# A hybrid SSD and attention layer on one core: silu moved to the projections and built from tanh, z loaded apart, group statistics taken a span later, a third product bank in the scan

## The chip, the core and the metric

The kernel runs on one core of a Trainium2 chip. The metric is the device time of one execution in microseconds; lower is better. The core's engines run side by side and meet through semaphores: TensorE (PE) multiplies matrices into the PSUM memory (8 banks of 512 float32 columns by 128 partitions), VectorE (DVE), ScalarE (ACT) and GpSimd (POOL) work elementwise, and SyncE (SP) issues the DMAs. Each engine takes its instructions in the order in which the built program has them.

## What is computed

One step of a layer for a 1024-frame prompt and a 64-frame continuation, laid side by side as T = 1088 columns. The parts that matter here:

```python
xn = _rmsnorm(x, p['norm_mix_w'])
proj = xn @ p['w_in']
z, xbc, dt_raw, q, k, v, gate_ssm, gate_att = jnp.split(proj, ...)
xbc_c, conv_new = _causal_dwconv(conv_past, xbc, p['ssm_conv_w'], p['ssm_conv_b'])
xbc_c = jax.nn.silu(xbc_c)
xs, bm, cm = jnp.split(xbc_c, ...)
y_ssm, ssm_new = _ssd_scan(xs, dt, a_neg, bm, cm, ...)      # chunk by chunk, 32 heads in 4 groups
y_ssm = y_ssm + p['ssm_d'] * xs
y_ssm = y_ssm * jax.nn.silu(z)
y_ssm = _rmsnorm(y_ssm by group, p['ssm_norm_w'])
o = differential attention over q, k, v (chunk-causal; the continuation sees 512 cached keys)
mix = sigmoid(gate_ssm) * (y_ssm @ w_branch_ssm) + sigmoid(gate_att) * (o @ w_branch_attn)
x = x + mix @ w_out
x = x + (silu(conv(h_a)) * h_b) @ w_down                     # h = RMSNorm(x) @ w_up
```

`silu(a)` is `a * sigmoid(a)`, which equals `(a/2) * (tanh(a/2) + 1)`.

## The kernel before, in words

**Products.** Every weight product is made from float32 numbers split into a high and a low part, as three matmuls per 128-row block (L148 to L150). One product of 128 output rows by 384 or 320 columns (the three parts of T in `WIDE`) is 24 matmuls and fills one PSUM bank. `acc` (L112) hands out the banks: two banks `mm` of the pool `pm`, and, while `more` is a pool, three further banks `mx`. `more` is set from L225 to L410, that is for the norm and for the projections of V, Q and K; after that there are two banks only. The piece that evacuates a bank must have read it to the end before the second-next product may begin in it.

**Stages.** First the norm of x and the projections of V and dt, then Q and K (`heads`, L312). When the 8 tiles of K are projected, `heads` scales all eight rows on DVE (L343 and L346), turns two of them by the rotary tables (L352 to L357), splits each into high and low (L307 and L308) and stores them. Beside this PE already works on the *stream* (`stream`, L465): the projections of z (`z_tiles`), of the convolution inputs x, B, C (`conv_tiles`) and of the gates (`gate_tiles`), in the order of `ORDER` (L67): four tiles of z, six of the convolution, sixteen of the gates, and so on. A z piece is copied from its bank by ACT (L429) and stored to `z_sc`. A convolution piece is copied by ACT into `pre` (L447), multiplied by the first tap (L456), three more taps follow on DVE (L458), and `cc` is stored to `x_sc`.

**Attention** (L483 to L642) goes head by head; each of its 72 units is followed by 1.9 pieces of the stream (`fill`). **The scan** (L645 to L774) runs over 12 spans: 4 groups by the 3 parts of T. `fetch` (L646) loads one span's B, C, four tiles of x and four of z into one tile `in`; `gate` (L655) applies silu to all ten, five at a time, on ACT (L658) and then loads the table set `natural_log_exp_and_others` (L660), which has Ln and Exp. `step` (L663) is one chunk of 128: the decays `bc` (a DMA that spreads 8 rows to all partitions, L668), transposes `tr` and `cb` on PE, Exp on ACT (L672, L687), the products `yi`, `ye` and the state update `stp`. `gated` (L717), at each span's end, adds the skip term, multiplies by the gated z on POOL, squares on ACT, sums on POOL, and then at once takes the group statistics with the ones matrix into a bank of its own, `gst` (L727), with Ln, Exp and Square on ACT (`rstd_of`, L206), the scaling on DVE (L731) and the store to `y_sc` (L732). The scan has six banks (`tr`, `cb`, `yi`, `ye`, `stp`, `gst`), each with one buffer. After every step and after `gated` 1.65 pieces are filled in: what is left of the stream, then, from the fifth span on, the attention branch product (`branch`, L161) and the first half of the SSM branch product. For the last chunk of each group the initial state is loaded at the place where it is needed (L695).

After the scan come the second half of the SSM branch (from groups 2 and 3 of `y_sc`), the output product with the second norm (L794 to L822, `rstd_of` again), and the feed-forward part, which is the rest of the time.

**Order.** The program is written with tiles in pools; a scheduler places the instructions of all engines. It takes the instructions roughly as written, evacuations and weight loads ahead of others (`tc.high_priority`), and moves an instruction up where its inputs come early. SP issues all DMAs in one queue.

## Time and profile before

| | us |
|---|---|
| median of 3 runs | 2575.67 |
| lowest, highest run | 2572.8, 2580.09 |
| the profiled execution, its own time | 2576.31 |
| span of the profiled execution (first to last instruction) | 2574.2 |
| PE busy in that span | 2525.0 |
| DVE, ACT, POOL busy | 1321.2, 1074.9, 288.3 |

"Busy" of PE is the union of its matmuls, which overlap; 15924 of them were recorded. The stages in the trace, by the time from the span's start: norm and V to about 100, Q and K to about 335, z and convolution alone to about 408, attention to about 1110, the scan to about 1600, the rest of the branches to about 1700, the output product to about 1790, the feed-forward part to the end. A row of the table of groups has the line, engine, operation, out<-in, partitions x elements and count, then busy microseconds and the mean nanoseconds of one, then the idle time of the engine just before.

### The profile page before, as it was taken

The page shows a single profiled execution, that of the slowest core. Times are in us where ns is not written, and L with a number is a line of the kernel's source. Part 1 is how long each engine was busy: PE and PEld are TensorE (multiplying, and loading weights), DVE is VectorE, ACT ScalarE, POOL GpSimd, SP SyncE. Part 2 cuts the span into 40 slices and gives each one's busy share as a digit, 9 for nine tenths or more (in the row PEclk, how much of TensorE's full clock was granted, in tenths as well). Part 3 has the DMA queues.
Part 4 walks back from the last instruction along what each step waited for, and adds up shares of the span by engine and source line. Part 5 has one row for each costly group of instructions (what it writes and reads, how often), then busy time and mean ns, then how long its engine had stood idle before and what let it go on. Part 6 is the DMA issues. An engine that isn't in the chain of part 4 may idle for free.

```text
span 2574.2 us, 40564 instructions
## 1 busy us (share of the span) xinstructions
PE 2525.0 (98%) x15924; PEld 2440.6 (95%) x15924; DVE 1321.2 (51%) x2238; ACT 1074.9 (42%) x2219; POOL 288.3 (11%) x393
## 2 busy tenths in 40 slices
PE   8999999999999999999989999999999999999999
PEld 8999998999999999988889889999999999999999
DVE  6326256655447674567556656657333333333333
ACT  6234344544445454478655664235313122221221
POOL 3000001000000110025233222022000000000000
PEclk9999999999999999999999999999999999999999
DMA  5217167545345434265795746666311111111111
GB/s 161 79 58 283 52 253 212 155 136 155 113 134 167 118 121 128 65 197 191 224 307 184 232 149 194 196 192 195 119 42 50 42 48 44 42 50 39 44 44 77
DMA packets 216352, 340.40 MB, mean 132 GB/s; under 512 B 28225, under 2 KB 164673, under 8 KB 216033
## 3 DMA queue, kind: packets, MB, share of 16 engines
q1 hardware_dynamic: 216160, 337.81, 41.7%
q8 instruction: 125, 2.05, 0.3%
q14 instruction: 67, 0.54, 0.1%
HBM read 237.60 MB, written 100.13 MB: 131 GB/s over the span
## 4 chain that ended last, share of the span: by engine, by line
PE 47%; DMA 5%; ACT 2%; DVE 1%; issue 1%; SPq 0%; POOL 0%; DVEq 0%; ACTq 0%; POOLq 0%
PE mm L148 8%; PE mm L150 8%; PE mm L149 8%; PE up L148 7%; PE up L149 7%; PE up L150 7%; DMA bc<-a_sc 1%; PE yi L692 1%; DMA b_f<-y_sc 1%; PE stp L705 1%; PE ye L699 1%; DMA in<-x_sc 1%; ACT bc L687 0%; DVE w_lo L142 0%; DVE b_lo L173 0%
## 5 line engine op out<-in xcount | busy, mean ns | idle before, releaser
L148 PE MATMUL mm<-xn_hi,w_hi 128*128 128x320 f32 (+1 forms) x1496 | 499.5, 334 | 5.1 <-ACT zr L429 4.1
L150 PE MATMUL mm<-xn_hi,w_lo 128*128 128x320 f32 (+1 forms) x1496 | 498.4, 333 | 0.0
L149 PE MATMUL mm<-xn_lo,w_hi 128*128 128x320 f32 (+1 forms) x1496 | 494.4, 331 | 0.0
L142 DVE TENSOR_TENSOR w_lo<-w_f,w_hi 128x1024 fp32r<-128x1024 f32 (+2 forms) x196 | 247.9, 1265 | 301.4 <-ACT w_hi L141 298.7
L141 ACT CAST w_hi<-w_f 128x1024 fp32r<-128x1024 f32 (+2 forms) x196 | 203.9, 1041 | 458.9 <-PE mm L149 297.5
L148 PE MATMUL up<-x_hi,w_hi 128*128 128x384 f32 (+1 forms) x1056 | 344.3, 327 | 1.3 <-ACT x_hi L821 1.3
L149 PE MATMUL up<-x_lo,w_hi 128*128 128x384 f32 (+1 forms) x1056 | 344.1, 326 | 0.0
L150 PE MATMUL up<-x_hi,w_lo 128*128 128x384 f32 (+1 forms) x1056 | 342.4, 326 | 0.0
L148 PEld LDWEIGHTS mm<-xn_hi,w_hi 128*128 128x128 f32 x1496 | 282.2, 189 | 11.7 <-ACT zr L429 5.0
L150 PEld LDWEIGHTS mm<-xn_hi,w_lo 128*128 128x128 f32 x1496 | 282.0, 188 | 3.8 <-issue 2.6
L149 PEld LDWEIGHTS mm<-xn_lo,w_hi 128*128 128x128 f32 x1496 | 282.2, 189 | 2.5 <-issue 1.2
L148 PE MATMUL mm<-b_hi,w_hi 128*128 128x384 f32 (+1 forms) x576 | 196.4, 341 | 9.1 <-ACT b_g L188 4.5
L148 PEld LDWEIGHTS up<-x_hi,w_hi 128*128 128x128 f32 x1056 | 198.1, 188 | 1.7 <-ACT x_hi L821 1.6
L149 PEld LDWEIGHTS up<-x_lo,w_hi 128*128 128x128 f32 x1056 | 198.2, 188 | 0.1
L150 PEld LDWEIGHTS up<-x_hi,w_lo 128*128 128x128 f32 x1056 | 198.0, 188 | 0.0
L150 PE MATMUL mm<-b_hi,w_lo 128*128 128x384 f32 (+1 forms) x576 | 193.2, 336 | 2.2 <-DVE w_lo L142 2.2
L149 PE MATMUL mm<-b_lo,w_hi 128*128 128x384 f32 (+1 forms) x576 | 192.7, 335 | 0.0
L881 DVE TENSOR_TENSOR xa<-xa,mm 128x384 f32<-128x384 f32 x144 | 76.5, 531 | 197.3 <-PE mm L150 197.3
L149 PE MATMUL mm<-f_lo,w_hi 128*128 128x384 f32 (+1 forms) x528 | 173.1, 328 | 0.0
L148 PE MATMUL mm<-f_hi,w_hi 128*128 128x384 f32 (+1 forms) x528 | 173.0, 328 | 0.0
L150 PE MATMUL mm<-f_hi,w_lo 128*128 128x384 f32 (+1 forms) x528 | 172.9, 328 | 0.0
L458 DVE SCALAR_TENSOR_TENSOR cc<-pre,par,cc 128x384 f32<-128x384 f32 (+1 forms) x216 | 128.4, 595 | 45.3 <-ACT cc L456 42.2
(253 smaller groups left out, 4741.0 us busy)
## 6 DMA issues: line engine op xcount, KB each, us to landing
w_f<-in_win_dram SPq DMA_DIRECT2D x76, 512.0 KB, 3.8
w_f<-in_wup_dram SPq DMA_DIRECT2D x44, 512.0 KB, 3.6
bc<-a_sc SPq DMA_DIRECT2D x32, 512.0 KB, 5.0
w_f<-in_wout_dram SPq DMA_DIRECT2D x24, 512.0 KB, 3.6
x_sc<-cc SPq DMA_DIRECT2D x48, 192.0 KB, 1.9
kh_t<-k_st SPq DMA_DIRECT2D x32, 272.0 KB, 7.9
kl_t<-k_st SPq DMA_DIRECT2D x32, 272.0 KB, 7.5
w_f<-in_wbs_dram SPq DMA_DIRECT2D x16, 512.0 KB, 4.5
```

What stands on the lines that cost most here:

```text
L141: S.copy(hi, w)
L142: V.tensor_tensor(out=lo, in0=w, in1=hi, op=ALU.subtract)
L148: PE.matmul(ps, a_hi, b_hi, start=i == 0, stop=False)
L149: PE.matmul(ps, a_hi, b_lo, start=False, stop=False)
L150: PE.matmul(ps, a_lo, b_hi, start=False, stop=i == n - 1)
L458: V.scalar_tensor_tensor(cc[:, :m], pre[:, i : i + m], cw(i), cc[:, :m], ALU.mult, ALU.add)
L692: PE.matmul(yi[u : u + 64, e // 2, :L], xdt[:L, e], bc[:L, e, :L], start=True, stop=True)
L699: PE.matmul(ye[:, j, :L], state[:, P * j : P * (j + 1)], bx[:, 1, cs], start=True, stop=True)
L705: PE.matmul(up, b_cb[:L, :P], xw[:L].rearrange("p e q -> p (e q)"), start=True, stop=True)
L881: V.tensor_tensor(out=xa[:, m, c : c + w], in0=xa[:, m, c : c + w], in1=ps, op=ALU.add)
```

## The change

1. **silu at the projections.** A z piece is no longer copied: ACT writes `tanh(z/2)` from the bank into `zr`, and a new DVE instruction makes `(zr + 1) * ps`, which reads the bank a second time. A convolution piece gets, after its taps, a Tanh on ACT (written into `pre`) and a DVE instruction `(pre + 1) * cc`. The convolution's taps and biases are halved beforehand and the norm weights of the SSM group norm are scaled to make up for z's factor 2 (`rstd_of` gets 0.25/512).
2. **No gate in the scan.** `gate`, with its Silu and its two table loads, is gone. z has a tile of its own, `zin`.
3. **Statistics a span later.** `gated` stops after the sums; the rest, `normed`, runs after the third step of the next span, and for the last span after the scan's last piece. Its bank is no longer `gst` but `cb`, which the steps use.
4. **A third product bank.** The bank that this frees becomes `mx`, a third bank of `acc` for the length of the scan.
5. `bc` has four buffers for three; the initial state is loaded once per group, when the group starts, into a tile `start`.

In the built program of after the table loads stand so: one before the first Tanh, Ln and Exp at the end of K's projection, then a pair (one for Ln, one for the Exp or Tanh behind it) at each of the 12 statistics of the scan, and a pair at each of the three statistics of the output product. The convolution and z pieces of the attention stage run Tanh beside Exp without a load.

```diff
@@ -45,7 +45,6 @@
 QR = 10
 QSQ = 1
 BF = 3
-GATE_AT = 2
 UPB = 5
 NXR = 4
 NSQ = 3
@@ -56,7 +55,6 @@
 ZR = 3
 ATT_STEPS = 1.9
 SCAN_STEPS = 1.65
-SPLIT = 5
 BRANCH_AT = 4
 
 
@@ -107,12 +105,13 @@
 
     pm = ctx.enter_context(tc.tile_pool(name="pm", bufs=2, space=PSUM))
 
-    more, at_bank = None, 0
+    more, at_bank = (None, 0), 0
 
     def acc(w):
         nonlocal at_bank
-        at_bank = (at_bank + 1) % 5
-        pool, tag = (more, "mx") if more is not None and at_bank < 3 else (pm, "mm")
+        pool, n = more
+        at_bank = (at_bank + 1) % (n + 2)
+        pool, tag = (pool, "mx") if at_bank < n else (pm, "mm")
         t = pool.tile([P, 512], F32, name=tag, tag=tag)
         return t[:, :w]
 
@@ -222,7 +221,7 @@
 
     s1 = ExitStack()
     ps1 = s1.enter_context(tc.tile_pool(name="ps1", bufs=1, space=PSUM))
-    more = s1.enter_context(tc.tile_pool(name="psx", bufs=3, space=PSUM))
+    more = s1.enter_context(tc.tile_pool(name="psx", bufs=3, space=PSUM)), 3
 
     def stat(w):
         t = ps1.tile([P, 512], F32, name="st", tag="st", bufs=3)
@@ -243,8 +242,8 @@
                     load(out=con, in_=cst)
             if x == 0:
                 load(out=par, in_=prm)
-                for a, b in ((O_MIX, O_CW), (O_SN, O_D), (O_QN, O_FW)):
-                    V.tensor_scalar_mul(par[:, a:b], par[:, a:b], -1.0)
+                for a, b, by in ((O_MIX, O_CW, -1.0), (O_CW, O_SN, 0.5), (O_SN, O_D, -0.5), (O_QN, O_FW, -1.0)):
+                    V.tensor_scalar_mul(par[:, a:b], par[:, a:b], by)
             for k in range(KT):
                 sq = nx.tile([P, max(NORM)], F32, name="nsq", tag="nsq", bufs=NSQ)
                 if k % 2:
@@ -407,7 +406,7 @@
             split_out(ck, j, PAST, c_st)
         heads(B_K, lambda j: col(O_KN + j), k_st, kT)
     s1.close()
-    more = None
+    more = None, 0
     ahead = AHEAD
     extra.release()
     extra = None
@@ -426,7 +425,8 @@
         for j in tiles:
             def evac(ps, c, w):
                 zr = staged("zr")[:, :w]
-                S.copy(zr, ps)
+                act(zr, ps, AF.Tanh, scale=0.5)
+                V.scalar_tensor_tensor(zr, zr, 1.0, ps, ALU.add, ALU.mult)
                 load(out=z_sc[P * j : P * (j + 1), c : c + w], in_=zr)
 
             yield from project(win[B_Z + j], evac)
@@ -456,6 +456,8 @@
                 act(cc[:, :m], pre[:, :m], AF.Identity, bias=col(O_CB + f), scale=cw(0))
                 for i in range(1, 4):
                     V.scalar_tensor_tensor(cc[:, :m], pre[:, i : i + m], cw(i), cc[:, :m], ALU.mult, ALU.add)
+                act(pre[:, :m], cc[:, :m], AF.Tanh)
+                V.scalar_tensor_tensor(cc[:, :m], pre[:, :m], 1.0, cc[:, :m], ALU.add, ALU.mult)
                 load(out=x_sc[P * f : P * (f + 1), c : c + n], in_=cc[:, :n])
                 if n < w:
                     load(out=x_sc[P * f : P * (f + 1), c + n : c + w], in_=cc[:, n + 3 : m])
@@ -643,28 +645,22 @@
 
 
     with tc.tile_pool(name="sp", bufs=1) as sp, tc.tile_pool(name="pss", bufs=1, space=PSUM) as pss:
+        more = pss, 1
         def fetch(g, c, w):
-            t = sp.tile([P, 10, 384], F32, name="in", tag="in", bufs=2)
+            t = sp.tile([P, 6, 384], F32, name="in", tag="in", bufs=2)
+            z = sp.tile([P, 4, 384], F32, name="zin", tag="zin", bufs=2)[:, :, :w]
             four = slice(4 * P * g, 4 * P * (g + 1))
             for u in range(2):
                 load(out=t[:, u, :w], in_=x_sc[P * (16 + 4 * u + g) : P * (17 + 4 * u + g), c : c + w])
-            for u, d in ((2, x_sc), (6, z_sc)):
-                load(out=t[:, u : u + 4, :w], in_=d[four, c : c + w].rearrange("(j p) t -> p j t", p=P))
-            return t
-
-        def gate(t, w, after=None):
-            with tc.issue_after(after.ins) if after is not None else ExitStack():
-                for u in range(0, 10, SPLIT):
-                    last = act(t[:, u : u + SPLIT, :w], t[:, u : u + SPLIT, :w], AF.Silu)
-            with tc.issue_after(last.ins):
-                S.preload_act_table_set(LN_EXP)
-            return t[:, 0:2], t[:, 2:6], t[:, 6:10, :w]
-
-        def step(g, ch, o, bx, xs, y, state):
+            for d, src in ((t[:, 2:, :w], x_sc), (z, z_sc)):
+                load(out=d, in_=src[four, c : c + w].rearrange("(j p) t -> p j t", p=P))
+            return t[:, 0:2], t[:, 2:6], z
+
+        def step(g, ch, o, bx, xs, y, state, start):
             L = P if ch < 8 else TS
             c0, cs = P * ch, slice(o, o + L)
             h8 = slice(8 * g, 8 * g + 8)
-            bc = sp.tile([P, 8, P], F32, name="bc", tag="bc", bufs=3)
+            bc = sp.tile([P, 8, P], F32, name="bc", tag="bc", bufs=4)
             load(out=bc[:, :, :L], in_=a_sc[h8, c0 : c0 + L].unsqueeze(0).to_broadcast([P, 8, L]))
             e2 = sp.tile([P, 4, P], F32, name="e2", tag="e2", bufs=2)
             for u in range(2):
@@ -684,15 +680,14 @@
             V.tensor_tensor(out=xx[:L], in0=tr3, in1=dtt[:L, :, ch, h8].unsqueeze(3).to_broadcast([L, 2, 8, 64]), op=ALU.mult)
             G.affine_select(bc[:L, :, :L], bc[:L, :, :L], [[0, 8], [1, L]], ALU.is_ge, -1e30, base=0, channel_multiplier=-1)
             for e in range(8):
-                last = act(bc[:L, e, :L], bc[:L, e, :L], AF.Exp, bias=nacum[:L, ch, 8 * g + e : 8 * g + e + 1])
+                act(bc[:L, e, :L], bc[:L, e, :L], AF.Exp, bias=nacum[:L, ch, 8 * g + e : 8 * g + e + 1])
             V.tensor_tensor(out=bc[:L, :, :L], in0=bc[:L, :, :L], in1=b_cb[:L, P : P + L].unsqueeze(1).to_broadcast([L, 8, L]), op=ALU.mult)
             yi = pss.tile([P, 4, P], F32, name="yi", tag="yi")
             for e in range(8):
                 u = 64 * (e % 2)
                 PE.matmul(yi[u : u + 64, e // 2, :L], xdt[:L, e], bc[:L, e, :L], start=True, stop=True)
             if ch == 8:
-                state = sp.tile([P, 512], F32, name="state", tag="state", bufs=2)
-                load(out=state, in_=st0[:, 512 * g : 512 * (g + 1)])
+                state = start
             if state is not None:
                 ye = pss.tile([P, 4, P], F32, name="ye", tag="ye")
                 for j in range(4):
@@ -712,43 +707,48 @@
                 V.tensor_tensor(out=new, in0=new, in1=up, op=ALU.add)
             if ch >= 7:
                 load(out=ssm[ch - 7, :, 512 * g : 512 * (g + 1)], in_=new)
-            return new, last
+            return new
 
         def gated(g, c, w, xs, zt, y):
-            rows = slice(4 * P * g, 4 * P * (g + 1))
-            part = lambda d: d[rows, c : c + w].rearrange("(j p) t -> p j t", p=P)
             for j in range(4):
                 V.scalar_tensor_tensor(y[:, j], xs[:, j, :w], col(O_D + 4 * g + j), y[:, j], ALU.mult, ALU.add)
             G.tensor_tensor(out=y, in0=y, in1=zt, op=ALU.mult)
             act(zt, y, AF.Square)
             G.tensor_tensor(out=zt[:, 0:2], in0=zt[:, 0:2], in1=zt[:, 2:4], op=ALU.add)
             G.tensor_tensor(out=zt[:, 0], in0=zt[:, 0], in1=zt[:, 1], op=ALU.add)
-            ps = pss.tile([P, 512], F32, name="gst", tag="gst")[:, :w]
+
+        def normed(g, c, w, xs, zt, y):
+            rows = slice(4 * P * g, 4 * P * (g + 1))
+            part = lambda d: d[rows, c : c + w].rearrange("(j p) t -> p j t", p=P)
+            ps = pss.tile([P, 512], F32, name="gst", tag="cb")[:, :w]
             PE.matmul(ps, ones, zt[:, 0], start=True, stop=True)
             rs = sp.tile([P, 384], F32, name="grs", tag="grs", bufs=2)[:, :w]
-            rstd_of(sp, rs, ps, w, "gn", 1.0 / 512)
+            rstd_of(sp, rs, ps, w, "gn", 0.25 / 512)
             for j in range(4):
                 V.scalar_tensor_tensor(y[:, j], y[:, j], col(O_SN + 4 * g + j), rs, ALU.mult, ALU.mult)
             load(out=part(y_sc), in_=y)
 
         def scan():
             spans = [(g, c, w) for g in range(4) for c, w in WIDE]
-            raw = fetch(*spans[0])
-            ready = [gate(raw, spans[0][2])]
+            got, due = [fetch(*spans[0])], None
             for i, (g, c, w) in enumerate(spans):
                 if c == 0:
                     state = None
+                    start = sp.tile([P, 512], F32, name="start", tag="start")
+                    load(out=start, in_=st0[:, 512 * g : 512 * (g + 1)])
                 if i + 1 < len(spans):
-                    raw = fetch(*spans[i + 1])
-                bx, xs, zt = ready[i]
+                    got.append(fetch(*spans[i + 1]))
+                bx, xs, zt = got[i]
                 y = sp.tile([P, 4, 384], F32, name="y", tag="y", bufs=2)
                 for o in range(0, w, P):
-                    state, last = step(g, (c + o) // P, o, bx, xs, y, state)
-                    if o == P * GATE_AT and i + 1 < len(spans):
-                        ready.append(gate(raw, spans[i + 1][2], last))
+                    state = step(g, (c + o) // P, o, bx, xs, y, state, start)
+                    if o == 2 * P and due is not None:
+                        normed(*due)
                     yield i
-                gated(g, c, w, xs, zt, y[:, :, :w])
+                due = g, c, w, xs, zt, y[:, :, :w]
+                gated(*due)
                 yield i
+            normed(*due)
 
         def stage():
             return bs.tile([P, 384], F32, name="b_f", tag="b_f", bufs=BF)
@@ -771,6 +771,7 @@
             fill(SCAN_STEPS)
         load(out=conv, in_=conv_o)
         run(filler)
+    more = None, 0
     dq.release()
```

## The prediction

> **What bounds the kernel now.** I read the page's head first, then the busy times by stretches of 100 us, then what PE waits for in the scan, then the clock in shorter stretches. The page:
>
> ```profile
> span 2574.2 us, 40564 instructions
> PE 2525.0 (98%) x15924; PEld 2440.6 (95%) x15924; DVE 1321.2 (51%) x2238; ACT 1074.9 (42%) x2219; POOL 288.3 (11%) x393
> ```
>
> PE is busy in all but 49.2 us. The profiled execution took 2576.31 us, 2.1 more than its span, and stands 0.6 above the median of 2575.67; the sum below is made against it. So an edit that takes time off ACT or DVE is worth only the PE idle time that it ends, and the PE clock that this idle time costs. Where that is, the stretches show (length, then busy us and instructions of PE, PEld, DVE, ACT, POOL, then the granted clock, DMA share and GB/s):
>
> ```profile
> 800.00:900.00 100.00, 100.00 (x646) 97.17 (x645) 71.47 (x152) 53.70 (x131) 11.08 (x37) 1.00 0.51 144
> 1100.00:1200.00 100.00, 96.81 (x655) 86.57 (x654) 70.66 (x88) 75.17 (x153) 39.14 (x33) 1.00 0.61 196
> 1200.00:1300.00 100.00, 94.25 (x622) 83.83 (x622) 58.96 (x68) 70.35 (x133) 36.73 (x25) 0.98 0.75 238
> 1300.00:1400.00 100.00, 93.19 (x619) 84.52 (x618) 58.84 (x82) 60.06 (x113) 30.20 (x21) 0.97 0.78 257
> 1400.00:1500.00 100.00, 90.72 (x559) 80.44 (x559) 62.55 (x86) 67.23 (x137) 27.21 (x19) 0.91 0.60 192
> 1500.00:1600.00 100.00, 99.90 (x660) 91.55 (x657) 66.16 (x90) 51.36 (x104) 30.36 (x19) 1.00 0.53 168
> 2000.00:2100.00 100.00, 100.00 (x606) 100.00 (x605) 36.30 (x57) 20.75 (x32) 2.65 (x8) 1.00 0.15 47
> ```
>
> In the feed-forward part PE is never idle: 606 matmuls in 100 us, so 165 ns from one to the next and 4.0 us for a product of 24. In attention it is nearly so, even where DVE is 71% busy. The scan, 1100 to 1600, holds 25.1 us of PE idle time, half of all there is. Who ended it (waits of PE from 1105 to 1615: us in total, times, longest):
>
> ```profile
> PE mm L148 <- ACT b_g L188: 4.5, 1, 4.5
> PE mm L148 <- ACT zr L429: 4.1, 4, 2.1
> PE ye L699 <- DMA state<-in_st_dram: 3.2, 2, 2.6
> PE mm L148 <- DVE b_g L190: 2.8, 1, 2.8
> PE tr L675 <- ACT in L658: 2.3, 3, 1.5
> PE stp L705 <- ACT b_cb L680: 1.9, 3, 0.9
> ```
>
> These are 18.8 us; eight smaller ones of that answer add 7.9, together 26.7. And the clock (stretches of 25 us, same columns; the ones with a clock under 1):
>
> ```profile
> 1225.00:1250.00 25.00, 21.13 (x135) 18.34 (x134) 15.08 (x21) 18.95 (x33) 7.05 (x5) 0.95 0.60 185
> 1250.00:1275.00 25.00, 25.00 (x163) 22.90 (x162) 13.55 (x16) 16.39 (x28) 8.12 (x7) 0.99 0.72 227
> 1300.00:1325.00 25.00, 19.81 (x130) 17.40 (x129) 11.48 (x18) 13.17 (x23) 3.25 (x5) 0.86 0.99 326
> 1425.00:1450.00 25.00, 20.86 (x131) 17.36 (x131) 20.00 (x32) 17.13 (x30) 2.65 (x2) 0.91 0.87 284
> 1450.00:1475.00 25.00, 25.00 (x155) 22.09 (x154) 11.97 (x21) 18.99 (x47) 11.41 (x7) 0.89 0.61 194
> 1475.00:1500.00 25.00, 20.47 (x125) 18.59 (x125) 11.32 (x16) 18.44 (x31) 3.80 (x4) 0.86 0.51 168
> ```
>
> The clock falls where PE stood idle for 4 us or more, and what it takes is 25 us times 0.05, 0.01, 0.14, 0.09, 0.11 and 0.14: 13.5 us. So at most 40 us can be won in the scan.
>
> **The change part by part.**
>
> *The gate goes (ACT in the scan).* The rows of ACT from 1105 to 1615, costliest first:
>
> ```profile
> L687 ACT ACTIVATE bc<-bc,nacum 128x128 f32<-128x128 f32 (+1 forms) x288 | 86.7, 384 | 19.2 <-POOL bc L685 18.7
> ...
> L658 ACT ACTIVATE in<-in 128x1920 f32<-128x1920 f32 (+1 forms) x24 | 40.6, 1714 | 1.5 <-DMA in<-x_sc 1.2 <-DMA in<-z_sc 0.2
> L658 ACT ACT_TABLE_LOAD x14 | 18.0, 1283 | 35.9 <-DMA in<-x_sc 35.9
> L660 ACT ACT_TABLE_LOAD x12 | 15.4, 1283 | 0.2
> ...
> L210 ACT ACTIVATE gn<-gst,eps_t 128x384 f32<-128x384 f32 (+1 forms) x12 | 6.7, 558 | 7.8 <-PE gst L727 7.7
> ```
>
> 40.6 us of silu leave ACT, and 26 table loads of 1.283 us. The 12 pairs of loads that the built program now has at the statistics put 24 back, so the loads cancel. But the lump goes: two silus and their two loads held ACT about 6.0 us at a time (2 x 1.714 + 2 x 1.283), and the copies that free the product banks, `zr` and `b_g`, and the copy `b_cb` queued behind it. I count the waits for b_g L188, zr, `in` and b_cb as ended by this: 4.5 + 4.1 + 2.3 + 1.9 = 12.8 us. What is late next in these places is the chain through `bc`, which the freer ACT shortens and the fourth buffer of `bc` starts earlier.
>
> *Early state:* the two waits for `state<-in_st_dram`, 3.2 us. Its DMA now stands on SP at the group's start and waits there for the previous group's last chunk to have read `start`; behind it wait that group's loads of `in` and `bc` and a weight block, all of which are wanted later. The load of `zin` likewise waits for the statistics of two spans before, with the same behind it. I cost both at nothing, as two loads of `bc` are ahead by then; if that lead is gone, it is the last rival's price. *Third bank:* an evacuation may be 4.0 us later than before; the one wait for b_g L190, 2.8 us, is shorter than that and goes. Ended in all: 18.8 of 26.7 us. The eight smaller ones (the state, weights, `bc`) I let stay. Of the clock I keep the loss at 1300 to 1325, 3.5 us, where the DMA share is 0.99, and take off the other 10.0. **Scan: -28.8 us.** Bounds: only the 4.5 and 2.3 that name silu's lump at first hand with half of the clock, about -10; all 40 us.
>
> *z's second pass at the end of K's projection.* This is the part that costs. The nearest rows for the new instructions: Tanh from a bank, the old copy, and the same DVE form from a bank:
>
> ```profile
> L420 ACT ACTIVATE gt<-mm 128x384 f32<-128x384 f32 x32 | 15.8, 493 | 31.7 <-PE mm L150 31.6
> L429 ACT COPY zr<-mm 128x384 f32<-128x384 f32 x32 | 15.1, 474 | 27.5 <-PE mm L150 17.6 <-issue 9.0 <-ACT p_t L557 0.8
> L190 DVE SCALAR_TENSOR_TENSOR b_g<-b_g,mm 128x384 f32<-128x384 f32 x16 | 8.8, 551 | 15.0 <-PE mm L150 10.8 <-DMA b_g<-g_sc 4.1
> ```
>
> The duration is nothing: 0.49 for 0.47 us on ACT and 0.55 on DVE. But the bank is now freed by DVE, and for z's first four tiles there are two banks and DVE is the engine that finishes K (time order, DVE):
>
> ```profile
> 342.26 7.67 DVE L343 SCALAR_TENSOR_TENSOR qr<-qr,par,qrs 128x1088 f32<-128x1088 f32 x6
> 349.85 2.61 DVE L346 SCALAR_TENSOR_TENSOR qr<-qr,par,qrs 128x1088 f32<-128x1088 f32 x2
> 352.37 1.28 DVE L308 TENSOR_TENSOR ql<-qr,qh 128x1088 fp32r<-128x1088 f32 x1
> 353.57 1.22 DVE L142 TENSOR_TENSOR w_lo<-w_f,w_hi 128x1024 fp32r<-128x1024 f32 x1
> ```
>
> In the built order of the changed program the DVE instruction of z's second piece stands ahead of these ten, that of the third behind them: 342.26 to 354.79 is 12.5 us in which no bank comes free. PE can spend 4.0 us of it on the fourth piece, in the bank that the second left; the fifth needs the third's bank and waits 12.5 + 0.5 - 4.0 = 9.0 us. Two later evacuations stand behind the rotary products and further splits, for which I add 1 us each. Such an idle stretch also drops the clock, as at 1475 to 1500, where 4.5 idle us go with 3.5 us of lost clock; part of that falls into the wait itself, and I take 2. **+13 us.** The order says the same: between the last statistics of K and the first score product it had 426 stream matmuls and has 344; 82 times 165 ns are 13.5 us. Below: 0 if the start of attention, which waits for K's stores, has as much slack; above: 18.
>
> *The rest of the pieces.* 72 convolution pieces get about 0.5 us of ACT and 0.55 of DVE, 48 z pieces 0.55 of DVE: some 65 us of DVE, most of it in attention, where 800 to 900 shows PE full at DVE 71%. The cover is the filler in PE's queue; bank holding doesn't change for the convolution. I take +2. If nothing covered it, each of some 80 pieces would cost its 0.55: +44; since PE idles not at all in 800 to 900, with DVE as full as it will be elsewhere, I keep 0 to 15. The one more scaling of parameters at the start, 120 columns once, I take at nothing.
>
> *Statistics later, and without the preloaded set.* Between spans nothing waits. Two places have nothing behind them: the last statistics of the scan, and the last of the output product, where PE waits already (waits of PE over the whole span, the first one for the rival below, then the chain of waits by time):
>
> ```profile
> PE sc L543 <- ACT p_t L557: 3.8, 1, 3.8
> ...
> PE up L148 <- ACT x_hi L821: 1.3, 1, 1.3
> ```
>
> ```profile
> 1598.95 5.79 DMA y_sc<-y
> 1604.81 3.19 DMA b_f<-y_sc
> ```
>
> Both chains get two table loads, 2.57 us, of which the first may fall in a gap of ACT: +2 at the output product, +3 at the scan's end, where the built order also has 8 matmuls fewer behind the statistics. Bounds 1 to 7 together. Here the Trainium skill speaks against the change. ScalarE: Activation LUTs, section "Table sets: the hidden batching unit", says that Ln and Exp share the set natural_log_exp_and_others, one load for both, and that calls are to be batched by set; the change gives up just that. Its section "What ACT_TABLE_LOAD costs" has 2.66 us for a switch with the drain, by which these two places would cost 5.3 us each and the forecast be some 5 us higher; the rows above have 1.283 and next to no idle time around it, and I go by them.
>
> **Sum:** -28.8 + 13 + 2 + 5 = -9 us: 2576.3 - 9 = **2567 us**, own range 2558 to 2575. (About 0.3%, 7.7 us, is what a measurement of this kernel can tell from no change.)
>
> **The rivals.**
>
> *The wait at K's end is hidden.* Attention's first scores wait for K's stores anyway, and among the waits is one of 3.8 us on `p_t`, at attention's start. If the idle time only takes their place, or all scan waits go, 9 to 20 us more are won: **2553**. Against it: the 82 matmuls that leave this stretch.
>
> *New waits in the scan.* The waits named were each ended by one engine, but the four-bank chain of transposes, decays and states is in one queue on PE, and the order is new. With half of the gain lost (14 us), the sum is +5: **2579**, no change.
>
> *The shared bank `cb` is held too long, and the kernel gets slower.* From the end of `gst` to the DVE instruction that reads the mean last the bank is taken: two loads 2.57, Ln, Exp and Square at 0.56 each, DVE 0.55, 4.8 us, and in the built order up to five Exps of 0.384 stand between: 6.7. The next `cb` transpose stands 32 to 79 stream matmuls later, which at 165 ns is 5.3 to 13 us, with two or three of the scan's own products beside. So it decides from a hold of some 7 us on: if ACT is kept by Exps whose `bc` lands late, PE stops in order, with all products behind it. 2.5 us at each of 11 spans are 27 us, which with the -9 gives +18: **2594**. For it: those Exps wait 18.7 us for `bc` by the row above; against it: most spans have 40 matmuls and more between, and ACT has 40 us less to do.
>
> **Chances.** Forecast 0.42, more won 0.15, no change by new waits 0.22, slower by the bank 0.21. The forecast's own range is on both sides of -0.3% (2568.6 from the profiled time): 0.27 of it below. Faster 0.45 with a little of the others, same 0.32, slower 0.23. The range leaves out the outer parts of the first and last rival: 2546 to 2590.
>
> **What would show it.** After should have: no wait for L658 or `state<-in_st_dram`; PE idle in the scan under 12 us; a wait of `mm` on DVE `zr` of some 9 us about 350 us after the start, with the clock under 1 behind it; `up <- x_hi` at 3 to 4 us. Waits of PE's `cb` on ACT or DVE `gn` would speak for the bank, waits of `po` or `sc` on DVE `cc` for a dearer attention; no PE idle time at 350 would fell the largest cost of the sum.

## The result, and the profile after

The changed kernel takes **2584.71 us** (median of 11 runs, 2580.46 to 2587.9), the kernel before 2575.67 (now 11 runs, of which the table above has the first three): the ratio is **1.0033, interval 1.0024 to 1.0042**. It is some 9 us slower, where 9 us faster was forecast. The page's head, to set beside that of before:

```profile
span 2581.3 us, 40809 instructions
...
PE 2520.2 (98%) x15924; PEld 2437.3 (94%) x15924; DVE 1381.9 (54%) x2359; ACT 1072.2 (42%) x2271; POOL 287.6 (11%) x393
```

PE now stands idle for 61.1 us instead of 49.2. Where, outside the scan, the changed kernel's stretches of 100 us show, with the same columns as before:

```profile
300.00:400.00 100.00, 90.35 (x532) 88.76 (x531) 51.32 (x76) 37.13 (x60) 0.29 (x2) 0.97 0.54 197
400.00:500.00 100.00, 97.08 (x611) 92.01 (x610) 79.30 (x171) 59.81 (x150) 10.47 (x34) 1.00 0.65 175
...
1700.00:1800.00 100.00, 93.88 (x558) 91.36 (x557) 64.56 (x86) 54.23 (x80) 31.14 (x22) 0.99 0.64 203
```

Of the kernel before, the stretch from 400 and the one from 1700, not shown yet:

```profile
400.00:500.00 100.00, 94.08 (x583) 89.33 (x582) 64.93 (x136) 48.77 (x125) 9.92 (x29) 0.98 0.68 178
...
1700.00:1800.00 100.00, 98.07 (x590) 96.61 (x589) 69.73 (x97) 48.46 (x79) 30.81 (x22) 1.00 0.64 202
```

The reader should compare the counts of matmuls, for a stretch with more of them has done more of the program. Where K ends, 300 to 400, 71 fewer; at attention's start, 400 to 500, 28 more; at the output product, 1700 to 1800, 32 fewer. In the scan, one stretch from 1105 to 1630 gives before and then after:

```profile
1105.00:1630.00 525.00, 497.54 (x3236) 448.31 (x3235) 333.00 (x443) 330.69 (x650) 163.22 (x114) 0.97 0.66 213
```

```profile
1105.00:1630.00 525.00, 496.49 (x3272) 450.73 (x3271) 358.37 (x487) 292.50 (x633) 161.50 (x116) 0.98 0.68 214
```

ACT has lost 38 us of work, but PE's idle time is 28.5 us where it was 27.5. The scan, where 29 us were to be won, does 36 matmuls more, which at 525/3236 = 162 ns each is some 6 us. What PE waits for in the changed kernel, over the whole span (us, times, longest), and then in the scan's stretch:

```profile
PE mm L147 <- DVE zr L429: 10.3, 3, 8.4
...
PE up L147 <- ACT x_hi L822: 3.9, 1, 3.9
```

```profile
PE stp L700 <- ACT b_cb L676: 4.6, 2, 2.7
PE mm L149 <- DVE w_lo L141: 4.1, 4, 1.9
PE mm L147 <- ACT b_hi L171: 2.9, 2, 2.0
PE mm L147 <- DVE b_g L189: 2.5, 1, 2.5
PE mm L148 <- DVE b_lo L172: 2.0, 1, 2.0
```

The waits for silu's `in` and for the state's DMA are gone as forecast; others of the same size stand in their place. Two that were counted as ended are still there: the one for ACT's `b_cb`, 4.6 us where it was 1.9, and the one for DVE's `b_g`, which the third product bank was to end, 2.5 us where it was 2.8 (L189 is L190 of before).

### The profile page after: what moved, and what is told of

Its sections match the earlier page's. It is cut to its first block, busy times and chain, and to the rows that moved or that the text cites. A ratio compares the mean times of both kernels' runs of the same rounds, so it can differ in the third digit from the quotient of the medians.

```text
span 2581.3 us, 40809 instructions
## 1 busy us (share of the span) xinstructions
PE 2520.2 (98%) x15924; PEld 2437.3 (94%) x15924; DVE 1381.9 (54%) x2359; ACT 1072.2 (42%) x2271; POOL 287.6 (11%) x393
## 4 chain that ended last, share of the span: by engine, by line
PE 68%; DVE 5%; DMA 5%; ACT 3%; issue 2%; SPq 1%; POOL 0%; DVEq 0%; ACTq 0%; POOLq 0%
PE mm L149 12%; PE mm L147 12%; PE mm L148 12%; PE up L147 7%; PE up L148 7%; PE up L149 7%; PE po L593 3%; PE sc L546 2%; PE sc L545 1%; PE pt L574 1%; DVE w_lo L141 1%; DMA b_f<-y_sc 1%; PE yi L688 1%; DVE y L728 1%; PE stp L700 1%
## 5 line engine op out<-in xcount | busy, mean ns | idle before, releaser
L147 PE MATMUL mm<-xn_hi,w_hi 128*128 128x384 f32 (+1 forms) x1416 | 472.7, 334 | 13.4 <-DVE zr L429 10.3
L149 PE MATMUL mm<-xn_hi,w_lo 128*128 128x384 f32 (+1 forms) x1416 | 470.8, 333 | 0.6 <-DVE w_lo L141 0.6
L148 PE MATMUL mm<-xn_lo,w_hi 128*128 128x384 f32 (+1 forms) x1416 | 468.7, 331 | 0.0
L147 PEld LDWEIGHTS mm<-xn_hi,w_hi 128*128 128x128 f32 x1416 | 267.5, 189 | 18.3 <-DVE zr L429 11.6
L149 PEld LDWEIGHTS mm<-xn_hi,w_lo 128*128 128x128 f32 x1416 | 267.3, 189 | 3.8 <-issue 1.9
L148 PEld LDWEIGHTS mm<-xn_lo,w_hi 128*128 128x128 f32 x1416 | 267.4, 189 | 2.8 <-issue 1.4
L147 PE MATMUL mm<-b_hi,w_hi 128*128 128x384 f32 (+1 forms) x448 | 149.6, 335 | 7.9 <-ACT b_hi L171 2.9
L149 PE MATMUL mm<-b_hi,w_lo 128*128 128x384 f32 (+1 forms) x448 | 148.1, 331 | 3.5 <-DVE w_lo L141 3.5
L148 PE MATMUL mm<-b_lo,w_hi 128*128 128x384 f32 (+1 forms) x448 | 148.1, 331 | 2.0 <-DVE b_lo L172 2.0
L559 ACT ACTIVATE p_t<-sc,mx 128x1024 f32<-128x1024 f32 (+5 forms) x144 | 106.2, 740 | 87.9 <-DVE mx L550 39.7
```

The source lines that it names most:

```text
L147: PE.matmul(ps, a_hi, b_hi, start=i == 0, stop=False)
L148: PE.matmul(ps, a_hi, b_lo, start=False, stop=False)
L149: PE.matmul(ps, a_lo, b_hi, start=False, stop=i == n - 1)
L559: act(p_t[:n, :nk], sc[c][:n, :nk], AF.Exp, bias=mx[:n, c : c + 1], accum_out=dst)
```

## The experiments

**Theory**: taking silu out of the scan wins there what was forecast or most of it, the ends of K's projection and of the output product cost what was forecast or more, and the statistics' new place (late, in the C.B bank, with the third product bank) takes the scan's gain back. **Rival**: the scan's waits are merely replaced, so that silu's removal wins nothing, whatever the statistics do. Times of different groups of runs are compared by their ratio to the kernel before, 0.1% being 2.6 us.

### The statistics' place, taken apart

*Silu alone* has parts 1, 2 and 5 of the change, with the statistics as before. Its edit, as all that follow, is against the changed kernel (`...` stands for lines left out):

```diff
-        more = pss, 1
...
-            ps = pss.tile([P, 512], F32, name="gst", tag="cb")[:, :w]
+            ps = pss.tile([P, 512], F32, name="gst", tag="gst")[:, :w]
...
-                    if o == 2 * P and due is not None:
-                        normed(*due)
...
                 gated(*due)
+                normed(*due)
                 yield i
-            normed(*due)
```

> The changed kernel with the group statistics taken at once again, in a bank gst of their own, and no third product bank in the scan; silu stays at the projections, z stays apart. Theory A (the scan's waits moved to DVE and DMA, whatever the banks): the scan is as long as in both others and the time within 4 us of 2584.7. Theory B (the new order with the shared bank took back what the missing silu gave): the scan loses 10 us or more of waits and the time is 2570 to 2576. Theory C (the third bank did help): it is slower, 2588 or more.

Measured: 2570.11 us, ratio 0.9976 [0.9967, 0.9985]. In the scan's stretch:

```profile
1105.00:1630.00 525.00, 507.33 (x3349) 460.35 (x3348) 351.89 (x501) 295.91 (x639) 160.41 (x116) 0.99 0.69 218
```

That is 113 matmuls more than before, 18 us. So the rival falls: silu's removal, together with part 5, from which no run parts it, wins in the scan, though 18 and not 29 us, for PE still idles 17.7 us there. The rest of the change loses it again. Four kernels part this rest.

*Late statistics alone* (a span later, bank of their own, no third bank): the changed kernel with

```diff
-        more = pss, 1
...
-            ps = pss.tile([P, 512], F32, name="gst", tag="cb")[:, :w]
+            ps = pss.tile([P, 512], F32, name="gst", tag="gst")[:, :w]
```

> silu_alone (2570.1) with the group statistics a span later, in a bank gst of their own, and no third product bank: the lateness alone. Theory L (the lateness holds z's tile and bunches the work of two spans, so that it costs what silu_alone won over the full change): 2580 to 2585. Theory B (the third bank or the shared bank cost it): 2568 to 2573.

*Shared bank alone*: silu alone with `tag="cb"`. *Third bank at once*: that with `more = pss, 1` too.

> silu_alone with the statistics at once, as there, but in the bank cb that the steps use, and no third product bank (one bank stays empty): the sharing alone. Theory C (PE waits for the mean to be read before the next transposes, the rival on the shared bank): 2578 or more, with waits of cb on DVE gn of some us. Theory B (the third bank): 2568 to 2573. Theory L: as theory B here.

> The changed kernel with the statistics at once: bank cb shared and the third product bank there, only the lateness taken away. Theory B (the third bank lets products run ahead of the scan's chain and of the weights): 2580 to 2585, with waits of products on w_lo, b_lo and b_hi as in the changed kernel. Theory L: 2568 to 2573. Theory C: 2578 or more and equal to shared_bank_only.

Measured: late statistics alone 2574.96 us, 0.9994 [0.9983, 1.0005]; shared bank alone 2593.27, 1.0072 [1.0055, 1.0089]; with the third bank 2600.64, 1.0099 [1.0082, 1.0116]. So lateness costs some 5 us (its interval just meets that of silu alone), which is between its two theories. The shared bank, with statistics at once, costs 25 us by the ratios, as theory C of its run had it. How, its waits in the scan's stretch and its stretch itself show:

```profile
PE mm L147 <- ACT b_hi L171: 13.1, 2, 11.9
PE gst L723 <- POOL zin L717: 8.0, 2, 5.9
PE cb L672 <- DVE gn L212: 5.2, 2, 3.7
```

```profile
1105.00:1630.00 525.00, 485.31 (x3198) 438.53 (x3196) 335.51 (x473) 292.46 (x632) 169.45 (x118) 0.96 0.66 208
```

PE stops in order at `gst`, whose sums POOL has not finished, and at the next `cb`, whose bank DVE has not read out; in silu alone, with a bank of its own, neither stands in that list. The largest wait, 13.1 us for `b_hi`, is taken up below. The view of the tile `cb` says who waited for it (us, times): silu alone first, then the shared bank.

```profile
who waited for it (us, times):
  ACT b_cb L675: 7.4, 7
```

```profile
who waited for it (us, times):
  ACT b_cb L675: 39.4, 18
```

ACT waits 39.4 us for the C.B products instead of 7.4. This is ACT's idle time and not yet time of the kernel: late statistics in the bank of `ye`, below, have 15.7 us of it and cost no more than late statistics in their own bank, which have 5.3. What it leads to is seen in PE's order. In silu alone the C.B products of 1 to 4 chunks of later spans stand ahead of the statistics of each span but the last. In shared bank alone none does, at any of the 12 spans: the next span can't start before the statistics of this one are out of the bank. The scan gets longer, its last statistics run at 1611.8 us instead of 1576.8, and by then PE has no other product ahead of those that need their result. The stretch behind, silu alone first, then the shared bank, and PE's longest wait in it:

```profile
1580.00:1655.00 75.00, 70.72 (x422) 69.07 (x421) 49.98 (x92) 20.80 (x36) 0.00 (x0) 1.00 0.68 209
```

```profile
1580.00:1655.00 75.00, 54.05 (x325) 47.66 (x324) 49.87 (x84) 23.64 (x40) 10.13 (x6) 0.89 0.47 151
```

```profile
1624.47 0.90 PE L147 MATMUL mm<-b_hi,w_hi 128*128 128x320 f32 x2 [11.91 <-ACT b_hi L171]
```

PE waits there for the last span's `y`, which goes through the statistics, the store to `y_sc` and the load back. Of the 24 us that PE idles more than in silu alone over the whole span (74.2 for 50.2), 16.7 lie in this stretch. With the third product bank at once the time is 7 us longer still, with intervals that overlap a little; theory C of that run had the two equal.

*Late and shared*: the changed kernel without its third bank (`more = pss, 1` taken out); one PSUM bank stays empty.

> The changed kernel without its third product bank alone: silu by tanh, z apart, statistics a span later, group statistics' products in the C.B bank; two product banks are used and one PSUM bank stays empty. It lies between two kernels already measured: late statistics with a bank of their own and no third bank 2575.0 us, the changed kernel 2584.7 us; 9.7 us are to be split between the shared bank and the third product bank. Theory A (the third product bank is what costs, since DVE and ACT get their products in another order and the pieces at the end of the scan wait): about 2575 to 2577 us, like late statistics alone. Theory B (sharing the C.B bank costs also a span later, the third bank nothing): about 2583 to 2586 us. Theory C (half and half): 2579 to 2581. In the at-once order the shared bank cost 23.2 us and the third bank another 7.3 us; if the third bank's price is the same here, 2584.7 - 7.3 = 2577.4 us.

Measured: 2590.92 us, 1.0055 [1.0038, 1.0071]. Theories A and C fall, and B is right of the bank and short of the price: it costs 16 us (0.0061 over late statistics alone) also a span later, and the third bank does not cost but gives some 6 back (the intervals of this kernel and the changed one overlap a little). Its stretch and waits there:

```profile
1105.00:1630.00 525.00, 493.25 (x3229) 446.74 (x3228) 357.73 (x480) 291.24 (x632) 163.88 (x116) 0.98 0.67 211
```

```profile
PE mm L147 <- DVE zr L429: 9.6, 6, 3.9
PE cb L672 <- ACT b_cb L675: 4.3, 2, 2.8
...
PE cb L672 <- DVE gn L212: 2.2, 1, 2.2
```

The loss is another here than with the statistics at once. It is not at the scan's end: from 1580 to 1655 PE idles 5.0 us, and 4.2 in late statistics alone; from 1105 to 1580 it idles 26.7 us where that has 16.0, and the mean clock is 0.97 for 0.99. Nor is it the lead of the next chunks, for three or four of them stand ahead of nearly all statistics in both. PE waits 2.2 us for the statistics to be read out of the bank and 4.3 us for `b_cb` to be copied out of it (2.8 in late statistics alone); longer than for either it waits for product banks, six times, 9.6 us (3.2 in late statistics alone). The longest of these stands in the time order of DVE (start, us, instruction, idle before):

```profile
1255.20 0.49 DVE L212 SCALAR_TENSOR_TENSOR gn<-gst,gn 128x320 f32<-128x320 f32 x1 [4.16 <-ACT gn L211]
1255.61 0.68 DVE L695 TENSOR_TENSOR y<-y,yi 128x512 f32<-128x512 f32 x1
1256.21 0.48 DVE L213 SCALAR_TENSOR_TENSOR grs<-gn,gn 128x320 f32<-128x320 f32 x1
1256.61 2.20 DVE L713 SCALAR_TENSOR_TENSOR y<-in,par,y 128x384 f32<-128x384 f32 x4
1258.72 5.11 DVE L727 SCALAR_TENSOR_TENSOR y<-y,par,grs 128x320 f32<-128x320 f32 x4
1263.75 0.54 DVE L429 SCALAR_TENSOR_TENSOR zr<-zr,mm 128x384 f32<-128x384 f32 x1
```

ACT's Tanh of that piece began at 1255.31; the bank came free at 1264.29. DVE had first stood 4.16 us for ACT's part of the statistics, and then had 8.5 us of other work ahead of this piece, 5.11 of them the four multiplications by `grs`, which the last section comes back to. Before the change ACT's copy freed a z bank, and such a burst on DVE held no z bank.

*Late, in another bank*: is it the C.B bank, or any bank that is used twice? Late and shared with `tag="ye"`, a bank which the next chunk wants after `cb`, without and with the third product bank:

> The changed kernel without the third product bank, its late group statistics in the bank of ye in place of the C.B bank; one PSUM bank stays empty. Measured neighbours: a bank of their own 2575.0 us, the C.B bank 2590.9 us. Theory A (it is the C.B bank: the next chunk's first products need it, ye's bank is wanted last): 2574 to 2579 us. Theory B (any shared bank costs, by the order that PE gets): 2586 us and more. Between: both have a part.

> The changed kernel with its late group statistics in the bank of ye in place of the C.B bank, third product bank kept: the change as it was, with one tag changed. If the third product bank is worth the 6 us that it was worth beside the shared C.B bank: 6 us under late_ye, 2568 to 2573 us if late_ye is near 2576. If the 6 us were only a repair of what the shared bank did: the same as late_ye.

Measured: 2574.88 us, 0.9999 [0.9990, 1.0008], and with the third bank 2575.21, 1.0001 [0.9993, 1.0010]. Theory A holds: in the bank of `ye` the statistics cost no more than in a bank of their own, and then the third product bank is worth nothing, so that its 6 us in the changed kernel were a repair of what the C.B bank did. The second of these kernels is the changed one with a single tag changed, and by the ratios it is 8 us faster. The stretch of the first has 91 matmuls more than late and shared:

```profile
1105.00:1630.00 525.00, 503.65 (x3320) 457.41 (x3319) 357.84 (x497) 295.21 (x636) 159.75 (x116) 0.99 0.68 217
```

### The end of K's projection

*Gates before z*: four of the gates' tiles stand ahead of z's first four, meant to keep every bank that DVE frees out of DVE's burst. *z in front of the scan*: the convolution's first tiles follow these gates, and most of z stands late in attention.

```diff
-ORDER = (("z", range(4)), ("c", group(0)), ("g", range(15, -1, -1)), ...
+ORDER = (("g", range(15, 11, -1)), ("z", range(4)), ("c", group(0)), ("g", range(11, -1, -1)), ...
```

```diff
+ORDER = (("g", range(15, 11, -1)), ("c", group(0)), ("z", range(4)), ("g", range(11, 7, -1)), ("c", group(1)),
+         ("c", group(2)), ("z", range(4, 16)), ("c", group(3)), ("g", range(7, 1, -1)))
...
-two = [z_tiles([j]) for j in (14, 15)]
+two = [gate_tiles([j]) for j in (1, 0)]
```

> The changed kernel with four of the sixteen gate tiles put ahead of the first four z tiles in the stream; nothing is added or left out. Gates are evacuated by ACT alone, so at the end of K's projection no bank waits for DVE. Theory A (the banks that z's second pass holds there cost time): the PE wait of 8.4 us on DVE zr near 350 us and the clock loss of about 3 us behind it go, and the time falls by 9 to 13 us, to 2572 to 2576. Theory B (attention's start waits for K's stores anyway, the wait only stands in for that): PE waits by as much at attention's start, and the time stays within 3 us of 2584.7.

> The changed kernel with the stream in another order: gates 15 to 12 first, all z tiles before the last convolution group, gates 7 to 0 last, in the scan. The 24 z evacuations by DVE leave the scan (about 13 us of DVE) and gates, evacuated by ACT alone, take their place. Theory A (DVE's added work in the scan took the place of the silu lumps): 5 to 12 us less than gates_before_z, 2562 to 2569. Theory B (the waits left in the scan hang on DMA and on the order): within 3 us of gates_before_z.

Measured: 2581.05 us, 1.0022 [1.0012, 1.0033], and 2571.89, 0.9982 [0.9973, 0.9991]. The stretches from 300 and 400 of gates before z:

```profile
300.00:400.00 100.00, 99.54 (x595) 98.00 (x595) 46.66 (x64) 37.72 (x61) 0.10 (x1) 1.00 0.56 207
400.00:500.00 100.00, 91.31 (x553) 86.36 (x553) 59.94 (x124) 46.17 (x118) 4.20 (x12) 0.95 0.66 172
```

The wait of 8.4 us is gone from the first stretch, but the second has 8.7 us of idle time, 4.1 of them for `zr` at another of DVE's bursts: 595 + 553 matmuls are 5 more than in the changed kernel. The wait was moved and not removed; the gain of some 3 us is near theory B. z in front of the scan has no wait for `zr` near K's end, and attention's own wait is back:

```profile
PE sc L545 <- ACT p_t L559: 5.3, 2, 4.0
```

Part of the wait at K's end thus stands in place of one of attention's. This kernel is 10 us faster than gates before z, as its theory A had it, and 13 us (0.0051) faster than the changed kernel. That is not K's end alone: from 300 to 500 it does 22 matmuls more than the changed kernel, 3.6 us, and in the scan's stretch 47 more (3319), 7.6 us. Whether the latter is DVE's lighter load there, as the theory says, no run parts from the new order.

### The table loads at the output product

*Table set once*: the changed kernel with the set of Ln and Exp loaded once, behind the first Square of the output product, for the statistics of all three parts; the trace has one load there, at 1697.67 us, in place of six. *Silu and table*: silu alone with the same. (Two of the expectations speak of four loads; both kernels have one.)

```diff
-                    act(s1_t, x, AF.Square)
+                    sq0 = act(s1_t, x, AF.Square)
+                    if c == 0:
+                        with tc.issue_after(sq0.ins):
+                            S.preload_act_table_set(LN_EXP)
```

> The changed kernel with one load of the set that has Ln and Exp, pinned behind the first Square of the output product, so that the three pairs of table loads at its statistics go. Theory A (these loads stand in the last chain before the feed-forward part): the PE wait of 3.9 us for x_hi falls to about 1.3, the clock drop behind it (6.8 us at half) goes, and the time falls by 3 to 6 us, to 2579 to 2582. Theory B (the loads lie in gaps of ACT): no change, 2583 to 2586.

> Silu by tanh and z apart alone (2570.1 us when measured before) with one preload of the table set of exp and ln for each of the four steps of the output product, pinned behind the first chunk's Square. The preload took 7.0 us off the changed kernel (2584.7 to 2577.8). If the table loads of the output product cost this kernel the same: 2563 to 2564 us, with the wait for x_hi near 1 us. If the gain came from another place in the changed kernel: 2568 to 2571 us.

Measured: 2577.76 us, 1.0010 [1.0001, 1.0019], and 2564.32, 0.9955 [0.9941, 0.9969]: 5.9 us (0.0023) and 5.4 us (0.0021), which agree. The time order of ACT in the changed kernel, and with the table set once:

```profile
1793.43 1.28 ACT L209 ACT_TABLE_LOAD   x1
1794.72 0.53 ACT L209 ACTIVATE n<-st,eps_t 128x320 f32<-128x320 f32 x1
1795.27 1.28 ACT L210 ACT_TABLE_LOAD   x1
1796.57 0.47 ACT L210 ACTIVATE n<-n 128x320 f32<-128x320 f32 x1
1797.07 0.47 ACT L211 ACTIVATE n<-n 128x320 f32<-128x320 f32 x1
```

```profile
1792.81 0.53 ACT L209 ACTIVATE n<-st,eps_t 128x320 f32<-128x320 f32 x1 [0.19 <-PE st L819]
1793.37 0.47 ACT L210 ACTIVATE n<-n 128x320 f32<-128x320 f32 x1
1793.88 0.47 ACT L211 ACTIVATE n<-n 128x320 f32<-128x320 f32 x1
```

The wait of PE for this, with the table set once:

```profile
PE up L147 <- ACT x_hi L825: 1.2, 1, 1.2
```

Two loads of 1.28 us go from this chain, and the wait for `x_hi` goes from 3.9 to 1.2 us. The rest of the gain goes with the clock: in the changed kernel it is 0.94 from 1780 to 1800 and 0.88 from 1800 to 1820, in this one 1.00 in both.

### Versions put together

*Combined*: silu alone, the order of z in front of the scan (the expectations call it two of z's steps first behind K), table set once. *Combined set*: the same with one load in the scan, at the first chunk of the third group, instead of the one at the output product. *Combined, ye, third bank*: that with late statistics in the bank of `ye` and the third product bank.

```diff
-                act(bc[:L, e, :L], bc[:L, e, :L], AF.Exp, ...)
+                ex = act(bc[:L, e, :L], bc[:L, e, :L], AF.Exp, ...)
+            if (g, ch) == (2, 0):
+                with tc.issue_after(ex.ins):
+                    S.preload_act_table_set(LN_EXP)
```

> silu_alone with the stream order of z_before_scan and the table set loaded once at the output product; nothing left out. If the three parts add up as measured one by one (-5.6 against before for silu_alone, -9.2 from gates_before_z to z_before_scan and -3.7 for gates first, -7 for the table set): 2570.1 - 12.8 - 7 = 2550. If the gain of the stream order came from the same waits that silu_alone already ended (theory of one pool of waits): 2559 to 2563.

> The combined kernel (silu by tanh, statistics at once in a bank of their own, two of z's steps first behind K) with one pinned preload of the table set of exp and ln behind the third step's Exps, in place of the four in the output product. It has 32 table loads where the combined kernel has 46; those that go are in the scan and in the output product, 14 x 1.283 us = 18 us of ACT. If ACT's pieces still end waits in the scan: 2550 to 2556 us. If the loads lie beside other work there: 2557 to 2561 us, like the combined kernel's 2558.8.

> The best kernel so far (2555.6 us: silu by tanh, two of z's steps first behind K, the table set of exp and ln preloaded once behind the third step's Exps) with the statistics a span later in the bank of ye and the third product bank, where that kernel has them at once in a bank of their own. If late statistics cost 5 us here too (2570.1 to 2575.0) and the third bank gives 6 back: 2553 to 2557 us. If the scan there has no product waits left for the third bank to end: 2558 to 2563 us.

Measured: 2558.78 us, 0.9934 [0.9917, 0.9950]; 2555.57, 0.9921 [0.9906, 0.9936]; 2565.67, 0.9964 [0.9951, 0.9978]. The first two beat both kernels, the best by 20 us against the kernel before. Combined falls 8 us short of the sum of its three parts (0.9902 by their ratios), near its second theory, by which the parts win from the same waits; which waits these are, no run shows. Whether the 13 table loads that the second has less in the scan give anything the intervals don't say. Late statistics cost 11 us here, although in the bank of `ye` and with the third product bank: the hope for 2553 to 2557 failed, and the time is above the other theory's 2558 to 2563 too.

The scan's stretch of the best kernel, combined set:

```profile
1105.00:1630.00 525.00, 514.46 (x3403) 469.53 (x3403) 351.58 (x487) 281.85 (x629) 163.55 (x116) 0.99 0.70 222
```

PE idles 10.5 us in it and does 167 matmuls more than before the change.

## Why the prediction was wrong, step by step

By the ratios the change comes apart as -6.2 us for silu with the gate gone, +4.6 for the late statistics, +15.7 for the C.B bank, -5.7 for the third product bank: +8.4, which is the measured 0.0033. The sizes belong to this order of steps: with the statistics at once the bank costs 25 us, and in the bank of `ye` the third product bank gives nothing.

- **The step that failed: "Between spans nothing waits".** *Statistics later* was costed at the two places behind which nothing stands, and the shared bank at nothing unless ACT's Exps came late. The runs show 15.7 us for the bank and about 4.6 for the lateness; with the 5.7 that the third product bank gave back they are 14.6 of the some 17 us between forecast (-9) and result (+8.4). The rest, to within an us or two, is the scan's term, 11 too hopeful, against K's end, 6 too dear.
- **The rival of the shared bank** named the right part with a chance of 0.21, at the wrong price (27 us) and by a mechanism that was not seen: PE was to stop at `cb`, and in the changed kernel waits there 0.2 us. With the statistics at once it does stop there (5.2 us), but most of the cost is the longer scan, which ends with nothing beside it; a span later the cost shows inside the scan, more than half of it as waits for late evacuations of products. How the second use of the bank leads to these stays open: the built orders differ in many places. That it is this bank is shown, by that of `ye`.
- **Scan, -28.8.** Mis-sized: silu alone wins 18 us there, by 113 matmuls. Of 27.5 us idle time 17.7 stayed, where under 12 was to be seen. The longest waits of silu alone there are 3.7 us of `cb` for ACT's `b_cb`, 2.5 for `b_g` (0.5 before), 2.1 for `w_lo` (2.2 before) and 2.0 for `zr`, now of DVE. So `b_cb` and `zr`, counted as ended, came back in another place or from another engine, and the small waits that were let stay did stay or grew. *Third bank*, costed within this term at 2.8 us, gave nothing where no bank was shared.
- **The rival of new waits** (half of the scan's gain lost) fits this: 11 of 28.8 us were. Its time does not follow from its sum, for 2576.3 + 5 is 2581 and not 2579.
- **K's end, +13.** Its mechanism was right: the wait for `zr` is 8.4 us (9.0 forecast), behind the very burst that was named:

```profile
344.69 7.66 DVE L342 SCALAR_TENSOR_TENSOR qr<-qr,par,qrs 128x1088 f32<-128x1088 f32 x6
352.27 2.61 DVE L345 SCALAR_TENSOR_TENSOR qr<-qr,par,qrs 128x1088 f32<-128x1088 f32 x2
354.79 1.28 DVE L307 TENSOR_TENSOR ql<-qr,qh 128x1088 fp32r<-128x1088 f32 x1
356.00 1.22 DVE L141 TENSOR_TENSOR w_lo<-w_f,w_hi 128x1024 fp32r<-128x1024 f32 x1
357.13 0.48 DVE L429 SCALAR_TENSOR_TENSOR zr<-zr,mm 128x320 f32<-128x320 f32 x1
```

  The size was not: 71 matmuls lost by 400 and 28 regained by 500 leave 43, at 165 ns 7 us. Attention's first wait for `p_t`, 3.8 us before, is gone; that much of the first rival was true.
- **The rest of the pieces, +2.** The changed kernel shows no wait of `po` or `sc` on `cc`, and from 500 to 1105 us, where most of these pieces stand, it does 3881 matmuls for 3884 before: half a us, with DVE busy 365 us instead of 344.
- **Table loads, +2 and +3.** The wait for `x_hi` is 3.9 us, as forecast at 3 to 4. But the term was the wait alone; with the clock that it takes the output product lost 5.4 to 5.9 us. For the scan's end nothing separates a cost. The Trainium skill's figure for a switch (ScalarE: Activation LUTs, "What ACT_TABLE_LOAD costs") is 2.66 us, of which 1.28 are the load and the rest a drain; the trace has the 1.28, with the next instruction 0.01 us behind, so that no time is left for a drain.

Without the wrong step, and with the other terms at what the runs measured, the sum is -18 + 7 + 0.5 + 5.6 = -5 us; silu alone, which is the change without that step, measured -6.

## What to carry to other kernels

When a tile moves into a bank that another step uses, ask which step needs the bank next and how early in its chunk: here the bank at the head of the chunk cost 16 us, one wanted later in it nothing. When an evacuation gets a second pass on another engine, look through that engine's queue for bursts, for a product bank is held until its last reader's turn. Here PE was 98% busy, and the waits that went were not won in full; count matmuls in the same stretch of before and after instead of adding waits.

## What the runs showed of the hardware

A DVE instruction can be held for the length of a POOL instruction beside it. The multiplications by `grs` (L728 in the changed kernel) have a median of 612 ns in the changed kernel and a longest of 3806; that one runs at 1258.19 beside this one on POOL, and it ends within 0.4 us of it:

```profile
1257.89 3.75 POOL L715 TENSOR_TENSOR y<-y,zin 128x1536 f32<-128x1536 f32 x1 [6.77 <-DVE y L714]
```

```profile
1257.73 5.19 DVE L728 SCALAR_TENSOR_TENSOR y<-y,par,grs 128x320 f32<-128x320 f32 x4
```

Of the 48 such instructions 11 have a POOL instruction beside most of their length, with a mean of 1662 ns, the other 37 one of 587 ns; before the change it was 2 of 48, in the bank of `ye` 20. The Trainium skill has this in SBUF — State Buffer, section "SBUF: two separate sides": DVE and GpSimd take a shared port pair as an exclusive lock for a whole instruction, also where DVE has two inputs in SBUF. The trace agrees. That the late statistics cost their 4.6 us by it, since their multiplications then stand beside POOL's gating of the next span, is argued and not shown: late in the bank of `ye` has 20 of them, late in a bank of its own 16, and the two take the same time.
